# Projecting all queries, keys and gates ahead of the attention in a two-layer hybrid decoder trunk

## Chip, cores and metric

One NeuronCore of a Trainium2 chip runs the whole program. The metric is device time in microseconds (us), the median of several executions. PE is TensorE, PEld its weight load, DVE VectorE, ACT ScalarE, POOL GpSimd, SP SyncE. All tensors are float32; matmuls take their operands as fp32r pairs (below).

## Reference

Two layers (DEPTH 2) over x of 1024 tokens by 1024 channels. Each layer, cut to what matters:

```python
h = rmsnorm(x, pre_g)
fq, fk, fv, ff, fg, dq, dk, dv, dg, cb, cc, cx, cg, mg = split(h @ w_in)
# fox: 8 heads of 64, causal, with a running sum c of log_sigmoid(ff + b_f)
y_fox = softmax(fq fk^T / 8 + c_q - c_k) fv * silu(fg)
# diff: 4 heads, two maps of 64 each, the first 16 of 64 dims rotated by position
y_diff = rmsnorm((softmax_0 - lam * softmax_1) dv) * (1 - lam_init) * silu(dg)
# conv: 3 taps along the tokens
y_conv = cb * conv(cc * cx) * silu(cg)
g = sigmoid(mg + b_m)                      # three times 1024 channels
m = g0 * (y_fox @ w_fox) + g1 * (y_diff @ w_diff) + g2 * (y_conv @ w_conv)
x = x + rmsnorm(m @ w_o, post_g)
```

## The kernel before

A float32 operand is held as two fp32r tiles, hi and lo (ACT copies hi, POOL or DVE subtracts to get lo), and each product is three matmuls (mm3, L346). The columns of w_in come in chunks of 128. A plain chunk over all 1024 tokens takes two halves (h) of 8 steps in the depth, times three: 48 matmuls of 512 columns. A Strassen pair (strassen, L483) computes two chunks from seven products of 4 x 3 matmuls each, 84 in place of 96; build_s (L434) makes the sums s1 to s4 of the quarters of h that this needs, and emit_pair (L304) the sums of the weights. The order of products in strassen is a11, a12, s2, s3, s1, a22, s4; each product has its own PSUM bank, and a function use(j, h, x, ps, own) takes each of the four results.

Four groups of PSUM banks are S (3), T (2), O (1) and F (2); bank() cycles through all eight, pF through F alone. SBUF tiles of 4 KB a partition come from one pool of 41 blocks (blk), smaller ones from five tmps. SP issues nearly all loads, in the order in which the program has them; ACT's queue issues the stores and small copies. The framework orders the work of the other engines from the program order and its own estimates. A small clock (Clock, L62) delays steps by due times so that ACT and DVE steps come behind the matmuls they depend on.

A layer (L1145) runs so. conv_pair for the first two chunks of each conv tensor takes cc and cx plain and, while they run, build_s; all else of the conv is in pairs, and so are the merge gates mg and the gate fg. conv_merge (L579) makes the third branch's gate and multiplies it at once with y_conv @ w_conv into m0 in DRAM; gates_spilled (L604) writes the other gates to DRAM. One quarter of h (a21), overwritten by then, is reloaded. A first v_unit (L622, values for two pairs of heads, h stationary, 256 weight columns moving, 8 token blocks of 24 matmuls) and a first qk_unit (L702) follow, with forget (L657) for the sums c.

Then the attention (L1009): eight windows, one for each fox head pair (FOX_ORDER) and then for each diff head. A window's units go through the query groups g = 1, 2, 3, 0; stage1 (logits, softmax) of a unit alternates with stage2 (transposes, product with v) of the one before. Beside it, interleave (L122) spreads a filling over the window in proportion to its cost; PLAN (L39) lists it: the qk_unit and v_unit of later windows, plain; dg plain and unactivated (gate_raw); y_prep (L1041), which loads an attention output and its gate and multiplies and splits them; merge_br (L1069), which multiplies a branch with its weights and its gate. A qk_unit keeps its tiles in SBUF as stacks of hi over lo; swap (L761) copies the queries with halves exchanged for each unit by small DMAs on ACT's queue, and for diff the rotation exchanges rows by DMA and multiplies with tables on POOL and DVE.

Behind the attention come the merges left over (five of the first branch, eight of the second), then the output projection in two halves (out_half, out_rows), which also prepares the next layer's h.

## Time and profile before

| | |
|---|---|
| median of 3 runs | 2552.33 us (2551.42 to 2553.53) |
| the profiled execution's own time | 2547.05 us |
| its span, first to last instruction | 2545.2 us |
| mean granted TensorE clock | 0.986 |
| DRAM traffic | 264.61 MB, mean 104 GB/s |

The span starts at the first instruction. Layer 0 holds its attention from 583 to 1106 us, layer 1 from 1850 to 2372 us. Busy times are of the union of an engine's instructions; matmuls are pipelined, so that one of 512 columns has a duration of about 0.4 us while the next starts 0.23 us after it. Some matmul records can be missing.

### The profile page before, as it was taken

How to read it: one execution, taken by the hardware profiler on the slowest of the kernel's cores; microseconds unless marked ns; L12 is line 12 of the kernel's file. 1: busy time of each engine (PE TensorE's matmuls, PEld its weight loads, DVE VectorE, ACT ScalarE, POOL GpSimd, SP SyncE). 2: the span in 40 equal slices, each digit the busy share in tenths (PEclk: the TensorE clock that was granted, in tenths of full speed). 3: DMA queues.
4: the chain of work that ended last, by engine and by line, in shares of the span. 5: the costliest groups of instructions: out<-in, count | busy, mean ns of one | idle time of the engine just before them, and what ended most of it. 6: DMA issues, size and time to landing. Idle time of an engine off the chain costs nothing. (4 is left out here: it accounts for less than half of the span.)

```text
span 2545.2 us, 35790 instructions
## 1 busy us (share of the span) xinstructions
PE 2427.9 (95%) x13112; PEld 2043.0 (80%) x13112; DVE 1620.5 (64%) x2889; ACT 1109.7 (44%) x2290; POOL 859.8 (34%) x621
## 2 busy tenths in 40 slices
PE   7899999999999999899997999999999999999998
PEld 5677888888989787678976778888889887877798
DVE  6966464446566877677588664344465678777764
ACT  4224334336565555443432242233365655555333
POOL 1566324421122223361025662344211122234600
PEclk9899999999999999999998999999999999999999
DMA  4012223342222222654521122233322222226534
GB/s 168 33 50 95 92 95 116 104 138 70 62 75 73 73 84 74 192 203 138 194 95 42 50 91 96 75 106 118 121 72 62 77 70 81 75 83 207 206 117 182
DMA packets 113343, 264.61 MB, mean 104 GB/s; under 512 B 16128, under 2 KB 41088, under 8 KB 113168
## 3 DMA queue, kind: packets, MB, share of 16 engines
q1 hardware_dynamic: 57584, 187.52, 21.6%
q10 hardware_dynamic: 55584, 74.80, 9.5%
q8 instruction: 104, 1.70, 0.3%
q14 instruction: 71, 0.58, 0.1%
HBM read 187.68 MB, written 55.71 MB: 96 GB/s over the span
## 5 line engine op out<-in xcount | busy, mean ns | idle before, releaser
L279 POOL TENSOR_TENSOR wlo<-wraw,whi 128x1024 fp32r<-128x1024 f32 (+2 forms) x93 | 199.9, 2152 | 596.0 <-ACT whi L276 510.5
L351 PE MATMUL F<-ht,wlo 128*128 128x512 f32 x792 | 329.5, 416 | 0.0
L352 PE MATMUL F<-ht,whi 128*128 128x512 f32 x792 | 316.3, 399 | 0.0
L353 PE MATMUL F<-ht,whi 128*128 128x512 f32 x792 | 316.3, 399 | 0.0
L319 POOL TENSOR_TENSOR wlo<-sw,whi 128x512 fp32r<-128x512 f32 x160 | 225.3, 1419 | 225.8 <-ACT whi L318 200.2
L319 POOL TENSOR_TENSOR wlo<-wraw,whi 128x1024 fp32r<-128x1024 f32 x80 | 158.9, 1988 | 186.8 <-ACT whi L318 186.7
L318 ACT CAST whi<-sw 128x512 fp32r<-128x512 f32 x160 | 96.0, 620 | 248.3 <-DVE sw L321 107.2
L822 DVE TENSOR_TENSOR pt<-T,pt 128x512 fp32r<-128x512 f32 (+1 forms) x240 | 147.9, 633 | 47.1 <-ACT pt L821 45.5
L353 PEld LDWEIGHTS F<-ht,whi 128*128 128x128 f32 x792 | 150.0, 189 | 31.3
L352 PEld LDWEIGHTS F<-ht,whi 128*128 128x128 f32 x792 | 151.3, 191 | 25.1
L351 PEld LDWEIGHTS F<-ht,wlo 128*128 128x128 f32 x792 | 151.1, 191 | 24.7
L276 ACT CAST whi<-wraw 128x1024 fp32r<-128x1024 f32 (+2 forms) x126 | 117.9, 938 | 116.0 <-PE F L353 37.7
L783 PE MATMUL S<-qk,qk 128*128 128x512 f32 (+2 forms) x384 | 141.0, 367 | 20.6 <-ACT p L935 20.5
L821 ACT CAST pt<-T 128x512 fp32r<-128x512 f32 (+1 forms) x240 | 125.4, 544 | 75.1 <-PE T L174 55.3
L935 ACT ACTIVATE p<-S,sm 128x512 f32<-128x512 f32 (+2 forms) x192 | 110.6, 581 | 78.7 <-DVE sm L931 39.5
L929 DVE TENSOR_REDUCE sm<-S 128x1 f32<-128x512 f32 (+2 forms) x192 | 104.2, 550 | 45.7 <-PE S L787 23.1
L174 PE MATMUL T<-ident,p 128*128 128x128 f32 x864 | 129.5, 274 | 3.4 <-DVE p L946 3.2
L784 PE MATMUL S<-qk,sw 128*128 128x512 f32 (+2 forms) x384 | 130.7, 345 | 0.0
L318 ACT CAST whi<-wraw 128x1024 fp32r<-128x1024 f32 x80 | 66.8, 835 | 145.1 <-PE S L353 42.5
L351 PE MATMUL F<-whi,ht 128*128 128x256 f32 (+1 forms) x416 | 122.8, 295 | 3.9 <-DVE vd L373 3.9
L855 ACT ACTIVATE p<-p,sm 128x384 f32<-128x384 f32 (+7 forms) x128 | 99.5, 777 | 57.7 <-DVE sm L848 47.0
L321 DVE TENSOR_TENSOR sw<-wraw,sw 128x512 f32<-128x512 f32 x80 | 70.0, 875 | 82.4 <-POOL wlo L319 81.8
(393 smaller groups left out, 7168.5 us busy)
## 6 DMA issues: line engine op xcount, KB each, us to landing
wraw<-wt SPq DMA_DIRECT2D x128, 512.0 KB
mg<-tmp ACTq DMA_DIRECT2D x64, 256.0 KB
sw<-qk ACTq DMA_DIRECT2D x256, 64.0 KB
g<-mg SPq DMA_DIRECT2D x32, 512.0 KB
wraw<-wo SPq DMA_DIRECT2D x32, 512.0 KB
x<-x SPq DMA_DIRECT2D x24, 512.0 KB
wraw<-wbr SPq DMA_DIRECT2D x48, 256.0 KB
m<-tmp ACTq DMA_DIRECT2D x32, 256.0 KB
```

The lines of the kernel that those rows point to most:

```text
L174: self.nc.tensor.transpose(out, x, self.ident)
L276: nc.scalar.copy(hi, raw)
L279: getattr(nc, eng).tensor_tensor(out=lo, in0=raw, in1=hi.bitcast(F32), op=ALU.subtract)
L318: nc.scalar.copy(w[0][:, o], f)
L319: nc.gpsimd.tensor_tensor(out=w[1][:, o], in0=f, in1=w[0][:, o].bitcast(F32), op=ALU.subtract)
L351: nc.tensor.matmul(ps, wl, xh, start=start and i == 0, stop=False)
L352: nc.tensor.matmul(ps, wh, xl, start=False, stop=False)
L353: nc.tensor.matmul(ps, wh, xh, start=False, stop=stop and i == n - 1)
L783: nc.tensor.matmul(ps[:, :wp], q[:, i * P:(i + 1) * P], k[:, c0:c0 + wp], start=True, stop=False)
L784: nc.tensor.matmul(ps[:, :wp], qsw[:, (i % 2) * P:(i % 2) * P + P], k[:, c0:c0 + wp], start=False, stop=not last)
L821: self.clock.later(0.1, lambda: nc.scalar.copy(hi, T[:, n0:]))
L822: done = self.clock.later(0.6, lambda: nc.vector.tensor_tensor(out=lo, in0=T[:, n0:], in1=hi.bitcast(F32), op=ALU.subtract))
```

## The change

In a layer, the four v_units come first, plain, and go to DRAM (L.v); build_s is cut in two steps that stand between them, and forget and, in layer 0, setup_late (the rotation tables) between the last two. Then all queries, keys, gates and the conv are projected in Strassen pairs, 32 of them; conv pairs alternate with the others. qk_pair writes hi and lo of the scaled results to DRAM by head (L.qk), for diff with columns gathered so that the 16 rotated dims of all heads stand in chunk 0, the only one that is rotated; the rotation runs behind the next pair's start. The third merge gate and y_conv go to DRAM too. strassen adds two more products into banks already used: a12's into that of a11, a22's into that of s3, s4's into that of s1. conv_merge, qk_unit, stack_evac, gate_raw, swap and the reload of a21 are gone.

In the attention the windows' filling is now a load_pair for the next window (ten DMAs, 4.2 MB: queries, queries with halves exchanged, keys, values), merges of the conv branch (br 2, the result to DRAM), y_preps and merges of the fox branch (br 0, which load the partial sum and write it back). One merge of br 0 and eight of br 1 stand behind the attention. The diff, cut:

```diff
 PLAN = (
-    (("qk", "f", 3),),
-    (("qk", "f", 0), ("v", "f", 0)),
-    (("qk", "f", 1),),
-    (("qk", "d", 0), ("v", "d", 0)),
-    (("qk", "d", 1), ("dg", 0)),
-    (("qk", "d", 2), ("v", "d", 1)),
-    (("qk", "d", 3), ("y", "f", 0), ("dg", 2), ("y", "f", 1), ("dg", 1), ("y", "f", 2), ("y", "f", 3)),
-    (("dg", 3), ("br", 0), ("br", 1), ("br", 2)),
+    (("load", "f", 1), ("br", 2, 0), ("br", 2, 1)),
+    (("load", "f", 2), ("br", 2, 2), ("br", 2, 3), ("y", "f", 0)),
+    (("load", "f", 3), ("br", 2, 4), ("br", 2, 5), ("y", "f", 1)),
+    (("load", "d", 0), ("br", 2, 6), ("y", "f", 2)),
+    (("load", "d", 1), ("br", 2, 7), ("y", "f", 3), ("br", 0, 0)),
+    (("load", "d", 2), ("br", 0, 1), ("br", 0, 2)),
+    (("load", "d", 3), ("br", 0, 3), ("br", 0, 4), ("y", "d", 0)),
+    (("br", 0, 5), ("y", "d", 1), ("br", 0, 6)),
 )
-FILLS = {f for w in PLAN for f in w}
-COST = {"v": 20.8, "qk": 20.8, "dg": 10.4, "y": 1.0, "br": 5.2}
+COST = {"load": 0.0, "y": 1.0, "br": 5.2}
...
+            yield
...
-    def strassen(self, L, c0, c1, use, uv=None):
+    def strassen(self, L, c0, c1, use, scale=1.0):
...
+        def product(b, a, ps=None):
+            more = ps is not None
+            ps = ps or self.bank()
+            self.mm3(ps, [(w[b][0][:, k], w[b][1][:, k], *(t[:, k % 2] for t in L.a[a][k // 2])) for k in range(4)],
+                     not more, True, True)
             return ps
...
+        uv = self.blk([P, 2, 512], F32, "uv")
+        u, v = uv[:, 0], uv[:, 1]
+        p1 = product("b11", "a11")
+        nc.scalar.activation(u, p1, AF.Copy, scale=scale)
+        p6 = product("t2", "s2")
+        self.plus(u, u, p6, scale)
+        use(0, 0, None, product("b21", "a12", p1), False)
+        p7 = product("t3", "s3")
+        self.plus(v, u, p7, scale)
         p5 = product("t1", "s1")
-        nc.vector.tensor_tensor(out=u, in0=u, in1=p5, op=ALU.add)
-        use(1, 1, v, p5, False)
...
+        use(1, 1, v, p5, True)
+        use(0, 1, u, product("t4", "a22", p7), False)
+        use(1, 0, u, product("b22", "s4", p5), True)
+
+    def plus(self, o, x, ps, scale=1.0):
+
+        if scale == 1.0:
+            self.nc.vector.tensor_tensor(out=o, in0=x, in1=ps, op=ALU.add)
+        else:
+            self.nc.vector.scalar_tensor_tensor(out=o, in0=ps, scalar=scale, in1=x, op0=ALU.mult, op1=ALU.add)
...
+        pair = lambda name, use: self.strassen(L, (name, c), (name, c + 1), use)
+        pair("cc", use_cc)
+        yield
+        pair("cx", times(u))
...
+        yield
+        pair("cb", times(t))
+        yield
+        pair("cg", use_cg)
+        for j in range(2):
             hi, lo = self.blk([P, S], F32R, "ych"), self.blk([P, S], F32R, "ycl")
-            self.split(hi, lo, t, self.nc.gpsimd)
-            L.yc.append((hi, lo))
-
...
+            self.split(hi, lo, t[j], nc.gpsimd)
+            for x, o in enumerate((hi, lo)):
+                nc.scalar.dma_start(L.yc[c + j, x], o.bitcast(F32))
+        yield
...
+            if t % 4 == 3:
+                for j in range(2):
+                    self.clock.later(0.5, lambda j=j, h=h: nc.scalar.dma_start(
+                        L.v[kind][2 * u + j, h], vt[j][h].rearrange("p t a d -> p (t a d)").bitcast(F32)))
...
+    def qk_pair(self, L, kind, n, c):
+
+        nc = self.nc
+        scale = -0.125 if n == "q" else 1.0
+        dst = L.qk[kind, n]
+
+        def store(ch, h, t):
             sl = slice(h * 512, h * 512 + 512)
+            for x in range(2):
+                src, d = t[:, x].bitcast(F32), dst[x]
+                if kind == "f":
+                    nc.scalar.dma_start(d[2 * ch:2 * ch + 2, :, sl].rearrange("m d s -> (m d) s"), src)
+                elif ch:
+                    nc.scalar.dma_start(d[:, 16 * ch:16 * ch + 16, sl], src)
+                else:
+                    for r in range(2):
+                        nc.scalar.dma_start(d[:, 8 * r:8 * r + 8, sl],
+                                            src[64 * r:64 * r + 64])
+
+        def use(j, h, x, ps, own):
+            y = self.total(x, ps, own, scale)
+            t = self.blk([P, 2, 512], F32R, "hl")
+            if kind == "d" and c + j == 0:
+                if x is None:
+                    y = self.tmp()
+                    nc.scalar.activation(y, ps, AF.Copy, scale=scale)
+                xs = self.tmp()
+                for r in range(2):
+                    nc.scalar.dma_start(xs[64 * r:64 * r + 64], y[64 - 64 * r:128 - 64 * r])
                 rt = self.blk([P, 2, 512], F32, "rope")
+                sl = slice(h * 512, h * 512 + 512)
                 nc.sync.dma_start(rt[:, 0], self.rope_c[:, sl])
                 nc.sync.dma_start(rt[:, 1], self.rope_s[:, sl])
+
+                def rotate():
+                    nc.gpsimd.tensor_tensor(out=xs, in0=xs, in1=rt[:, 1], op=ALU.mult)
+                    nc.vector.tensor_tensor(out=y, in0=y, in1=rt[:, 0], op=ALU.mult)
+                    nc.vector.tensor_tensor(out=y, in0=y, in1=xs, op=ALU.add)
+                    self.split(t[:, 0], t[:, 1], y)
+                    store(c + j, h, t)
+
+                self.behind.append(rotate)
+                return
+            if x is None and scale != 1.0:
+                nc.scalar.activation(t[:, 0], ps, AF.Copy, scale=scale)
+                nc.vector.scalar_tensor_tensor(out=t[:, 1], in0=ps, scalar=scale, in1=t[:, 0].bitcast(F32),
+                                               op0=ALU.mult, op1=ALU.subtract)
+            else:
+                self.split(t[:, 0], t[:, 1], y)
+            store(c + j, h, t)
+
+        self.strassen(L, (kind + n, c), (kind + n, c + 1), use, scale)
...
+    def load_pair(self, L, kind, p):
+
+
+        nc = self.nc
+        L.q[kind, p], L.k[kind, p], L.vt[kind, p] = [], [], []
+        for e in range(2):
+            m = 2 * p + e
+            tiles = [self.blk([P, S], F32R, "qk") for _ in range(3)]
+            for t, n in zip(tiles, "qk"):
+                nc.sync.dma_start(t.bitcast(F32), L.qk[kind, n][:, m])
+            for x in range(2):
+                nc.sync.dma_start(tiles[2][64 - 64 * x:128 - 64 * x].bitcast(F32), L.qk[kind, "q"][x, m])
+            L.q[kind, p].append((tiles[0], tiles[2]))
+            L.k[kind, p].append(tiles[1])
         for h in range(2):
+            t = self.blk([P, 4, 4, 64], F32R, f"v{kind}")
+            nc.sync.dma_start(t.rearrange("p t a d -> p (t a d)").bitcast(F32), L.v[kind][p, h])
+            L.vt[kind, p].append(t)
+        L.done.add((kind, p))
...
-    def swap(self, qs, g):
-
-        nc = self.nc
-        s = self.sw(F32R)
-        gs = slice(g * 256, g * 256 + 256)
-        out = [s[:, i * 256:i * 256 + 256] for i in range(2)]
-        for t, q in zip(out, qs):
-            nc.scalar.dma_start(t[0:64].bitcast(F32), q[64:128, gs].bitcast(F32))
-            nc.scalar.dma_start(t[64:128].bitcast(F32), q[0:64, gs].bitcast(F32))
-        return out
...
-            nc.tensor.matmul(ps[:, :wp], qsw[:, (i % 2) * P:(i % 2) * P + P], k[:, c0:c0 + wp],
+            nc.tensor.matmul(ps[:, :wp], qsw[:, i * P:(i + 1) * P], k[:, c0:c0 + wp],
...
-            q, k, cb = L.qk["f", p][0][e], L.qk["f", p][1][e], L.cb[hd]
-            if e == 0:
-                L.fsw = self.swap(L.qk["f", p][0], g)
-            qsw = L.fsw[e]
+            (q, qsw), k, cb = L.q["f", p][e], L.k["f", p][e], L.cb[hd]
...
-            if raw:
-                later(0.0, lambda g1=g1: nc.scalar.activation(g1, g1, AF.Sigmoid))
-                later(0.6, mul)
-            later(1.0, lambda o1=o1, hi=hi: nc.scalar.copy(hi, o1))
-            y.append(later(1.6, lambda o1=o1, hi=hi, lo=lo: nc.gpsimd.tensor_tensor(
+            later(0.7, lambda o1=o1, hi=hi: nc.scalar.copy(hi, o1))
+            y.append(later(1.3, lambda o1=o1, hi=hi, lo=lo: nc.gpsimd.tensor_tensor(
                 out=lo, in0=o1, in1=hi.bitcast(F32), op=ALU.subtract)))
             yield 0.5
...
-        if br == 0:
+        if br != 2:
             mf = self.blk([P, S], F32, "mf")
-            nc.sync.dma_start(mf, L.m0[dc])
-            L.mf.append(mf)
+            nc.sync.dma_start(mf, L.m0[br][dc])
...
+        if br != 1:
+            self.clock.later(1.8, lambda: nc.scalar.dma_start(L.m0[0 if br == 2 else 1][dc], g))
...
+        self.behind = []
+        sums = self.build_s(L)
         run(self.v_unit(L, "f", 1, self.bank))
+        next(sums)
+        run(self.v_unit(L, "f", 0, self.bank))
+        run(sums)
         self.clock.flush()
-        decay = self.forget(L)
...
-        L.done = {("qk", "f", 2), ("v", "f", 1)}
+        run(self.v_unit(L, "d", 0, self.bank))
+        run(self.forget(L))
+        if l == 0:
+            self.setup_late()
+        run(self.v_unit(L, "d", 1, self.bank))
+        self.clock.flush()
+
+        def pairs(names, fn):
+            return [lambda n=n, c=c: fn(n, c) for n in names for c in (0, 2)]
+
+        qk = pairs(("fq", "fk", "dq", "dk"), lambda n, c: self.qk_pair(L, n[0], n[1], c))
+        silu = pairs(("fg", "dg"), lambda n, c: self.gates_spilled(L, (n, c), (n, c + 1)))
+        gates = [lambda c=c: self.gates_spilled(L, ("mg", c), ("mg", c + 1))
+                 for b in (16, 0, 8) for c in range(b, b + 8, 2)]
+        rest = qk + silu + gates
+        conv = chain([self.conv_pair(L, 0), self.conv_pair(L, 2)])
+        for n, job in enumerate(rest):
+            if n % 2 == 0:
+                next(conv, None)
+            self.run_behind()
+            if n == len(rest) - 2:
+                self.load_pair(L, "f", 0)
+            job()
+        run(conv)
+        self.load_yc(L)
...
-                p = FOX_ORDER[n]
-                units = [self.fox_unit(L, p, e, g) for g in G_ORDER for e in range(2)]
+                units = [self.fox_unit(L, n, e, g) for g in G_ORDER for e in range(2)]
...
+                if f[0] == "load":
+                    gens.append(self.loads(L, *f[1:]))
...
-                    gens.append(self.merge_br(L, 0, f[1], self.pF))
...
+                    gens.append(self.merge_br(L, f[1], f[2], self.pF))
...
+        for c in range(len(L.y["d"]), 4):
+            run(self.y_prep(L, "d", c))
+        done = {f for w in PLAN for f in w}
         for br in range(2):
...
+                if ("br", br, dc) not in done:
                     run(self.merge_br(L, br, dc, self.bank))
...
+    def chunk(n, c):
+        if n not in ("dq", "dk"):
+            return cols(OFF[n] + c * P, P)
+
+        m, d = np.arange(8), np.arange(16)
+        i = m[:, None] * 64 + c * 16 + d[None, :]
+        i = i.reshape(8, 2, 8).transpose(1, 0, 2) if c == 0 else i
+        return w[:, :, OFF[n] + i.reshape(-1)]
```

## Rows read from the trace of the kernel before

**Rows 1.** The page's part 1: busy us, share of the span, instructions.
```profile
PE 2427.9 (95%) x13112; PEld 2043.0 (80%) x13112; DVE 1620.5 (64%) x2889; ACT 1109.7 (44%) x2290; POOL 859.8 (34%) x621
```

**Rows 2.** Windows: stretch, length, each engine's busy us (instructions), granted clock, DMA share, GB/s.
```profile
250.00:500.00 250.00, 250.00 (x1083) 203.70 (x1082) 125.84 (x184) 94.96 (x137) 97.25 (x65) 1.00 0.30 103
...
75.00:250.00 175.00, 158.10 (x651) 126.02 (x651) 129.98 (x129) 54.36 (x80) 111.73 (x66) 0.96 0.16 57
1300.00:1500.00 200.00, 182.30 (x748) 145.84 (x747) 153.68 (x140) 58.23 (x84) 118.34 (x66) 0.94 0.16 55
```

**Rows 3.** Waits of PE, 75 to 250 us: who, for whom, us, times, longest.
```profile
PE F L351 <- POOL wlo L319: 5.4, 2, 3.4
PE S L351 <- ACT s L448: 5.1, 1, 5.1
```

**Rows 4.** Windows of the attention: single ones of layer 0, then the halves of both layers.
```profile
831.00:893.00 62.00, 59.24 (x319) 47.54 (x318) 51.27 (x118) 36.15 (x95) 15.65 (x16) 1.00 0.26 75
...
965.00:1046.00 81.00, 76.77 (x394) 62.48 (x393) 63.90 (x121) 40.93 (x103) 33.94 (x26) 0.98 0.40 117
1046.00:1106.00 60.00, 51.99 (x262) 40.22 (x261) 38.33 (x92) 28.04 (x78) 21.89 (x20) 0.94 0.55 181
...
583.00:831.00 248.00, 247.11 (x1636) 216.71 (x1635) 163.08 (x445) 146.56 (x326) 44.17 (x53) 1.00 0.25 72
831.00:1106.00 275.00, 255.87 (x1411) 208.88 (x1410) 207.17 (x451) 144.53 (x378) 88.13 (x77) 0.98 0.36 111
1850.00:2098.00 248.00, 246.65 (x1633) 216.32 (x1633) 162.95 (x445) 146.33 (x326) 43.65 (x51) 1.00 0.25 72
2098.00:2372.00 274.00, 256.12 (x1419) 210.26 (x1418) 207.94 (x452) 146.66 (x380) 88.21 (x77) 0.99 0.36 112
```

**Rows 5.** Timeline of PE in a v_unit: start, us, line, tile; eleven matmuls, first and last.
```profile
701.42 0.28 PE L352 MATMUL F<-wlo,ht 128*128 128x256 f32 x1
...
702.60 0.28 PE L353 MATMUL F<-whi,ht 128*128 128x256 f32 x1
```

**Rows 6.** DVE by line: the second window, the fifth, the last, then the run.
```profile
L699 DVE SCALAR_TENSOR_TENSOR qk<-F,qk 64x512 fp32r<-64x512 f32 x8 | 5.5, 689 | 0.9 <-ACT qk L698 0.7
...
L699 DVE SCALAR_TENSOR_TENSOR qk<-tmp,qk 64x512 fp32r<-64x512 f32 x8 | 5.5, 687 | 0.3
L732 DVE TENSOR_TENSOR tmp<-tmp,tmp 128x512 f32<-128x512 f32 x4 | 4.3, 1086 | 0.0
...
L728 DVE TENSOR_TENSOR tmp<-tmp,rope 128x512 f32<-128x512 f32 x4 | 2.7, 676 | 0.0
...
L1058 DVE TENSOR_TENSOR o<-o,g 128x512 f32<-128x512 f32 x5 | 3.3, 700 | 6.6 <-issue 6.6
...
L1058 DVE TENSOR_TENSOR o<-o,g 128x512 f32<-128x512 f32 x48 | 50.1, 1093 | 14.0 <-issue 6.6 <-DMA g<-fg 5.6 <-ACT g L1061 1.7
...
L1087 DVE TENSOR_TENSOR g<-g,F 128x512 f32<-128x512 f32 x26 | 17.6, 681 | 10.7 <-PE F L353 10.7
...
L373 DVE TENSOR_TENSOR vf<-F,vf 128x128 fp32r<-128x128 f32 x40 | 11.6, 289 | 17.3 <-ACT vf L372 17.0
```

**Rows 7.** Timeline of ACT in the fifth window: a DMA issue on its queue.
```profile
851.60 0.69 ACTq L723 DMA_DIRECT2D tmp<-tmp  x1
```

**Rows 8.** Windows: the merges behind the attention, layer 0 and layer 1.
```profile
1106.00:1186.00 80.00, 75.73 (x333) 61.40 (x332) 63.84 (x76) 29.71 (x47) 42.96 (x30) 0.98 0.58 205
2372.00:2449.00 77.00, 73.91 (x315) 59.68 (x314) 61.67 (x73) 26.75 (x45) 42.96 (x29) 0.96 0.56 203
```

**Rows 9.** Windows: two neighbouring stretches at the end of the attention of layer 0.
```profile
1040.00:1060.00 20.00, 18.00 (x87) 13.83 (x86) 9.34 (x21) 10.17 (x26) 11.15 (x11) 0.98 0.76 232
1060.00:1080.00 20.00, 15.09 (x73) 11.08 (x71) 14.87 (x39) 9.74 (x29) 3.27 (x4) 0.85 0.53 166
```

**Rows 10.** Waits of SP's queue over the run: who, for whom, us, times, longest.
```profile
SPq L878 <- DVE pt L822: 198.6, 4, 51.5
```

More of the change, by code (lines that the diff above doesn't have):

```diff
@@ L505, in plain @@
-    def plain(self, L, jobs):
-        for i in range(0, len(jobs), 3):
-            part = [(self.load_chunk(L.l, *c), use) for c, use in jobs[i:i + 3]]
-            for h in range(2):
-                for q, (w, use) in enumerate(part):
-                    if (i, h, q) == (3, 0, 0):
-                        self.build_s(L)
-                    use(h, self.proj(w, h))
-    def total(self, x, ps, own):
+        def product(b, a, ps=None):
[3 more added lines that the diff above has]
+                     not more, True, True)
+            return ps
@@ L1001, in stage2 @@
             later(2.0, out)
[L1003 to L1007 removed]
+        return stage1, stage2, 2 * W1D * (4 * g + 3) + W2D * (g + 1), {("d", hd)}
     def attention(self, L, windows):
@@ L1024, in attention @@
         fill = windows[0][1]
-        for _ in range(3):
-            next(fill, None)
         run(stage1(0))
@@ L1142, in out_rows, with run_behind, loads @@
                 nc.scalar.dma_start(self.x1[(h * 4 + tb) * P:(h * 4 + tb + 1) * P, :], xt)
+    def run_behind(self):
+        jobs, self.behind = self.behind, []
+        for fn in jobs:
+            fn()
+    def loads(self, L, kind, p):
+        self.load_pair(L, kind, p)
+        yield 0.0
     def layer(self, l):
@@ L1164, in layer @@
-        gates = [(n, c) for n in ("mg", "fg", "dg") for c in range(16 if n == "mg" else 4) if (n, c) not in FILLS]
-        gates = list(zip(gates[::2], gates[1::2]))
-        for pair in gates[:2]:
-            self.gates_spilled(L, *pair)
-        late = self.setup_late() if l == 0 else iter(())
-        for dc in range(0, 8, 2):
-            if dc >= 4:
-                next(late, None)
-            self.conv_merge(L, dc)
-        run(late)
-        for pair in gates[2:]:
-            self.gates_spilled(L, *pair)
```

196 lines of the change are left out of this document (37 added, 159 removed).

## Prediction

> **What bounds the kernel now.** I read the page's first line first: TensorE (PE) is busy 2427.9 of 2545.2 us, VectorE (DVE) 1620.5, ScalarE (ACT) 1109.7 [rows 1]. So PE's work decides, but a share over the whole run hides the stages; the stretches come next. In the steady part of the projections PE issues 1083 matmuls in 250 us, 0.23 us each, with DVE at half load [rows 2]: a matmul saved there is worth 0.23 us. Early in each layer PE falls short: 651 instructions in 175 us and 748 in 200 us, where 0.23 us each would need 150 and 172 us [rows 2]; it waits there for the splits of weights and of the Strassen sums [rows 3]. Then the attention, 248 + 275 = 523 us in layer 0 and 248 + 274 = 522 us in layer 1. Its eight windows show two regimes: in the four fox windows PE is busy 247 of 248 us with DVE at 66%; in the fifth and the seventh DVE is at 83 and 79% and PE falls 3 to 4 us short [rows 4]. That is the row to remember: projections inside the attention give PE something to do while the softmax chain is under way.
>
> **Part 1: matmuls removed.** Per layer 24 chunks are plain (4 in the first conv_pair, 16 queries and keys, 4 dg), 48 matmuls each. As 12 Strassen pairs of 84 they lose 12 x 12 = 144 matmuls, 288 in all: 66 us at 0.23 us. Nothing else on PE changes in count. The 66 us are the whole prize; the rest is a question of where work lies.
>
> **Part 2: the attention gets shorter, and poorer in filling.** What leaves it in a layer: seven qk units of 96 matmuls less the 18 already issued ahead of it (654), four dg chunks (192), three merges (72), so 918 x 0.23 = 211 us; and three v units of 192 matmuls of 256 columns at (702.60 - 701.42)/10 = 0.118 us [rows 5], 68 us. What comes in: 15 merges of 24 matmuls, 360 x 0.23 = 83 us. By PE alone 523 - 196 = 327 us. Now the same for DVE. It is busy 163 + 207 = 370 us there [rows 4]. Leaving: three f units of 8 x 0.689 = 5.5 us; four d units of 5.5 + 4.3 + 2.7 = 12.5 us; three v units of 16 x 0.29 = 4.6 us, together 80 us [rows 6]. Coming: 12 more merges of 2 x 0.68 us and two more y_prep of 2 x 0.70 us, 19 us [rows 6]. Left: 309 us. DVE would have to be busy 95% of 327 us, which no stretch of the attention shows. The fifth window has 51.27 of 62 us, 83%, at full speed of the rest; the seventh 63.90 of 81, 79%, also with transfers in its way [rows 4]. Against these stands what goes: the swaps (16 small DMA issues a window) and the rope exchange, each holding ACT's queue up to 0.7 us [rows 7], and GpSimd's large weight splits, beside which DVE's SBUF operations stretch (the multiply at L1058: 1.09 us over the run, 0.70 us in the last window, where POOL does less [rows 6]). I take 88%, near the good end because that traffic goes: 309/0.88 = 351 us. Ends: 327 us (PE alone) and 309/0.79 = 391 us. Gain: 172 + 171 = 343 us, between 391 and 263.
>
> **Part 3: the stage before the attention gets longer.** Per layer it loses the plain conv (192 matmuls), conv_merge's own matmuls (192), one plain qk unit and the 18 matmuls ahead (114), and its pairs go from 20 to 32: 2688 against 2178, +510 x 0.23 = 117 us. Three v units come in, 68 us. +185 us a layer, +371 us in all, if PE runs at its steady pace. Does cover hold? A pair takes PE 84 x 0.23 = 19.3 us; in the steady row DVE, ACT and POOL are busy 126, 95 and 97 of 250 us [rows 2], so splits, the new scaled copies and stores (each 0.3 to 0.7 us of ACT's queue) fit. The banks p1, p7 and p5 are now written again; each reader has one product between, 12 x 0.23 = 2.8 us, against a read of 0.7 us. If DVE came later than that, 64 pairs would each pay; at 0.7 us apiece 45 us. The stalls early in the layer (25 + 28 us, from rows 2) should shrink: build_s now has three v units (68 us of PE) beside it rather than a stage that already used DVE for 130 of 175 us. I take two thirds of them, -35 us; ends 0 and -53. Against that: v_unit on the first half of the rows offers PE 96 x 0.118 = 11 us before the second half must be there, where three plain chunks offered 72 x 0.23 = 17 us, so up to 5 us a layer, I take 5 in all; and setup_late comes as one block, 3 us (ends 0 and 10). forget keeps its place in the chain and its cost.
>
> **Part 4: behind the attention.** Nine merges instead of thirteen: 4 x 24 x 0.23 = 22 us less per layer of the 80 and 77 us [rows 8]. But only one merge of the first branch (5.5 us) is left to cover the way of the last head's output through DRAM, where five covered it; y_prep has one multiply fewer. +3 us a layer (ends 0 and 8). Together -38 us.
>
> **Traffic.** Everything now goes through DRAM. In the attention an estimate from the diff: seven pair loads of 4.2 MB, rows of c 4.2, gates, weights and partial sums of the merges 23, y_prep 8, outputs 4: 70 MB in 351 us, 200 GB/s. The stretch behind the attention already runs at 205 GB/s and 58% [rows 8], so it fits, without much room.
>
> **The sum.** -343 + 371 - 35 + 5 + 3 - 38 = -37 us. The profiled execution took 2547.05 us with its span of 2545.2; the median of the three runs is 2552.33. From the median: 2515 us.
>
> **Rivals.**
> *PE alone sets the attention.* With DVE rid of stretched operations 327 us a layer holds: 2 x 24 us better, 2466 us. For it: in the fox windows PE is hardly ever idle [rows 4]. Against: they had 22 to 45 us of filling each for 25 to 30 us of attention; now it is 5 to 11 us.
> *The softmax chain sets the attention, and the kernel gets slower.* If the windows run at the seventh's 79% of DVE, the attention takes 391 us a layer, 2 x 40 us more than I said: 2595 us. It decides from 351 + 37/2 = 370 us, DVE at 83.5%, which is just above what the fifth window reached with more filling. For it: one S bank in three is held until ACT's exponential is done, and the remaining filling comes in two pieces a window.
> *The gate queues behind the pair.* SP issues load_pair first, then the gate of the window's first merge. 4.2 MB at the 232 GB/s of [rows 9] are 18 us; the first merge's half is done some 3 us into the window, so DVE, which takes its instructions in order, could stand 15 us at the multiply and the banks would fill behind it. In all 14 windows 210 us, 2725 us; it decides from three of them (37/15). Against: that multiply never waited for its gate, its idle time is all PE's; only y_prep's waited for one, 5.6 us over the run [rows 6]. SP's queue does stand: 198.6 us at the cB load, for a block to come free [rows 10]. The Trainium skill, DMA: Bandwidth & Descriptors, section "Queues, rings and completion order", says that SP has one ring on each DMA engine and that descriptors are taken in ring order, which speaks for this rival; no row here shows a gate late because of it.
> *The clock falls.* In the window stretch 1060 to 1080, after PE had been busy 18 of 20 us, it was busy 15 of 20 and the granted clock was 0.85, a mix of 2.4 and 1.2 GHz; over the last window it was 0.94 [rows 9, 4]. If all of the attention ran at 0.94, 6% of 351 us twice would be lost, 42 us: 2557 us, no change. The Trainium skill, TensorE: Matmul & The Clock Gate, section "Why this matters for your kernels", warns of idle stretches between bursts of matmuls, since the engine then drops to half its clock; by that the thinner filling costs as this rival says, and by the row of the fifth window (clock 1.00 at 95% busy) nothing. I sum with nothing.
> *The change does not do what it says*: the saved matmuls come back as waits for re-used banks, the 45 us above. It would lie between no change and the slower case, and is counted there.
>
> **How the numbers follow.** My forecast, 2480 to 2547 us: 0.50. PE alone, below 2480: 0.17. No change, the clock or the banks: 0.09. The softmax chain: 0.17. The gate: 0.07. About 0.2% (5 us) is what a measurement of this kernel can tell, so faster is 0.67, same 0.09, slower 0.24. The range 2450 to 2590 leaves out the lower end of the PE case (0.05), the upper end of the chain case (0.08) and the gate (0.07).
>
> **What would show it.** Right: 288 fewer matmuls of 512 columns; a stage before the attention of some 750 us in layer 0, PE full after the first 120; attention windows of about 40 us (fox) and 47 us (diff), DVE between 85 and 90% in them; DRAM traffic near 200 GB/s there. Wrong: windows over 46 us on average with DVE under 83% (chain); DVE or PE waiting for a DMA at the merges (gate); granted clock under 0.95 through the attention; PE waiting for DVE or ACT inside strassen. My weakest number is the 88%: two points of it are 16 us.

## The result, and the profile after

The changed kernel takes 3298.61 us (median of four, 3291.04 to 3302.33) against 2552.93 us in the same session: 1.292 times as long (95% interval 1.289 to 1.294). I had forecast 2515 us, within 2450 to 2590. Sign and size are both wrong.

The page of the changed kernel: busy time by engine, the bytes moved, and the group with the longest idle time on DVE.

```profile
PE 2478.9 (75%) x12824; PEld 2048.8 (62%) x12824; DVE 1590.5 (48%) x2897; ACT 1085.9 (33%) x2292; POOL 920.5 (28%) x677
...
HBM read 271.56 MB, written 127.01 MB: 121 GB/s over the span
...
L1045 DVE TENSOR_TENSOR g<-g,F 128x512 f32<-128x512 f32 x69 | 46.1, 678 | 452.5 <-DMA g<-mg 444.8
```

The 288 matmuls are gone, as counted (13112 to 12824, [rows 1]). PE is idle a quarter of the time, and one multiply, a merge's product by its gate, stands 445 us for the gate's load.

To see where, I cut both kernels at the first and the last score matmul (S) of each attention. Windows: stretch, length, busy us of each engine (instructions), granted clock, DMA share, GB/s. The last stretch, behind the attention of layer 1, stands in the table alone. First after:

```profile
0.00:832.40 832.40, 750.12 (x3528) 618.52 (x3529) 435.71 (x570) 274.01 (x468) 367.48 (x232) 0.97 0.37 125
832.40:1492.80 660.40, 340.15 (x1854) 269.65 (x1853) 284.14 (x766) 216.07 (x551) 77.53 (x94) 0.74 0.34 105
1492.80:2463.20 970.40, 897.55 (x4562) 752.21 (x4562) 496.41 (x652) 323.70 (x589) 381.38 (x244) 0.97 0.39 133
2463.20:3124.90 661.70, 339.33 (x1856) 269.66 (x1855) 284.52 (x767) 215.96 (x551) 77.77 (x95) 0.75 0.35 105
```

The same stretches of the kernel before:

```profile
0.00:583.00 583.00, 547.49 (x2442) 446.27 (x2443) 346.15 (x439) 209.93 (x321) 252.87 (x156) 0.99 0.28 98
583.00:1090.20 507.20, 488.29 (x2961) 413.68 (x2960) 359.63 (x873) 283.94 (x683) 126.78 (x124) 0.99 0.31 91
1090.20:1849.60 759.40, 726.28 (x3598) 608.03 (x3597) 439.98 (x542) 263.56 (x454) 304.93 (x187) 0.98 0.31 109
1849.60:2354.40 504.80, 486.67 (x2960) 413.46 (x2959) 359.21 (x873) 284.04 (x683) 126.65 (x124) 0.99 0.30 92
```

My sum, put on these borders (in the attentions 507.2 - 172 and 504.8 - 171; each stage ahead +185.5 - 17.5 + 2.5, the first +3 more; -19 behind each attention), beside what was measured. The columns e3, e6 and e5 are experiments below.

| stretch | before | forecast | after | e3 | e6 | e5 |
|---|---|---|---|---|---|---|
| ahead, layer 0 | 583.0 | 756.5 | 832.4 | 787.4 | 784.0 | 786.7 |
| attention, layer 0 | 507.2 | 335.2 | 660.4 | 460.6 | 396.7 | 366.6 |
| between | 759.4 | 910.9 | 970.4 | 922.2 | 921.6 | 924.0 |
| attention, layer 1 | 504.8 | 333.8 | 661.7 | 462.6 | 403.4 | 368.4 |
| behind | 190.8 | 171.8 | 171.4 | 170.9 | 171.4 | 171.0 |
| span | 2545.2 | 2508.2 | 3296.3 | 2803.7 | 2677.1 | 2616.7 |

Of the 788 us between forecast and result 653 lie in the two attentions and 135 ahead of them. PE and DVE together are far from full there: PE 340 and DVE 284 of 660 us, at 105 GB/s. Something that is neither work nor volume sets the time. The waits name it: who waits for whom, us, times, longest; PE, then DVE, then ACT.

```profile
PE F L349 <- DVE g L1045: 439.6, 13, 49.0
PE S L747 <- ACT p L896: 130.2, 12, 33.8
...
DVE g L1045 <- DMA g<-mg: 445.6, 12, 49.5
...
DVE sm L901 <- ACT p L896: 132.6, 16, 33.3
...
DVE sw L318 <- DMA wraw<-wt: 63.2, 7, 28.5
...
ACT whi L273 <- DMA wraw<-wbr: 580.8, 18, 49.3
```

It is one chain: the gate and the weights of a merge come late; DVE and ACT stand at them in their own order, and the exponentials and bank reads behind them stand too. And why late? SP's queue in the first window of layer 0: start, us, instruction (L721, L723 and L728 are load_pair; L268 a merge's weights; L1033 its gate).

```profile
829.08 0.55 SPq L721 DMA_DIRECT2D qk<-qf  x1
...
830.57 11.95 SPq L723 DMA_DIRECT2D qk<-qf  x2
...
843.24 10.92 SPq L721 DMA_DIRECT2D qk<-kf  x1
854.25 11.78 SPq L723 DMA_DIRECT2D qk<-qf  x2
866.12 3.24 SPq L728 DMA_DIRECT2D vf<-vf  x2
869.46 1.71 SPq L268 DMA_DIRECT2D wraw<-wbr  x1
871.26 1.59 SPq L1033 DMA_DIRECT2D g<-mg  x1
```

The gate is issued 42 us after the pair's first load, because three of these rows hold SP 11 to 12 us each. That is not so elsewhere: 53 of SP's 591 DMA issues take more than 4 us in this run, 48 of them for queries and keys, and none of 407 does in the kernel before. And in the middle of that, with every compute engine at rest:

```profile
850.00:860.00 10.00, 0.00 (x0) 0.00 (x0) 0.00 (x0) 0.00 (x0) 0.00 (x0) 0.50 0.18 57
```

57 GB/s with nothing but loads from SP's queue under way, where the merges of the kernel before ran at 205 [rows 8]. The DMA share of 0.18 is 2.9 of 16 engines. So these loads are slow by themselves, not for want of bandwidth; why, the experiments must show.

Two theories go from here. *Narrow*: load_pair reads both halves of a head's queries in one DMA, from a source of shape 2 x 64 x 1024 into 128 partitions, and that shape uses few engines. *Order*: the loads are as fast as others, but too much stands in SP's queue ahead of the merges (my rival "the gate queues behind the pair").

The Trainium skill, DMA: Bandwidth & Descriptors, section "Why a DMA increments its semaphore by 16 and not by 1", says that a transfer is spread over the largest number of engines, up to 16, that divides the slowest dimension other than 1 of both its sides; for a slowest dimension of 2 that is two engines. By it the narrow theory holds, and the 2.9 engines of the row lie near it (two for the narrow loads; the pair's loads of 64 partitions, which are not of that shape, stand between them). No row here counts the engines of one load.

### The profile page after: what moved, and what is told of

Its sections match the earlier page's. It is cut to its first block, busy times and chain, and to the rows that moved or that the text cites. A ratio compares the mean times of both kernels' runs of the same rounds, so it can differ in the third digit from the quotient of the medians.

```text
span 3296.3 us, 35531 instructions
## 1 busy us (share of the span) xinstructions
PE 2478.9 (75%) x12824; PEld 2048.8 (62%) x12824; DVE 1590.5 (48%) x2897; ACT 1085.9 (33%) x2292; POOL 920.5 (28%) x677
## 5 line engine op out<-in xcount | busy, mean ns | idle before, releaser
L316 POOL TENSOR_TENSOR wlo<-sw,whi 128x512 fp32r<-128x512 f32 x256 | 351.1, 1382 | 399.4 <-ACT whi L315 399.1
L276 POOL TENSOR_TENSOR wlo<-wraw,whi 128x512 fp32r<-128x512 f32 (+2 forms) x61 | 100.9, 1656 | 1052.1 <-ACT whi L273 1021.4
L316 POOL TENSOR_TENSOR wlo<-wraw,whi 128x1024 fp32r<-128x1024 f32 (+1 forms) x128 | 239.0, 1867 | 340.3 <-ACT whi L315 338.2
L315 ACT CAST whi<-wraw 128x1024 fp32r<-128x1024 f32 (+1 forms) x128 | 107.0, 836 | 316.9 <-issue 107.9
L349 PE MATMUL S<-s,wlo 128*128 128x512 f32 x448 | 179.1, 400 | 10.0 <-POOL wlo L316 8.8
L747 PEld LDWEIGHTS S<-qk,qk 128*128 128x128 f32 x384 | 80.4, 209 | 164.1 <-ACT p L896 140.9
L351 PE MATMUL S<-s,whi 128*128 128x512 f32 x448 | 178.6, 399 | 0.0
L350 PE MATMUL S<-s,whi 128*128 128x512 f32 x448 | 177.9, 397 | 0.0
L349 PE MATMUL T<-ht,wlo 128*128 128x512 f32 x384 | 154.3, 402 | 30.5 <-ACT uv L491 30.2
L351 PE MATMUL T<-ht,whi 128*128 128x512 f32 x384 | 152.3, 396 | 0.0
L350 PE MATMUL T<-ht,whi 128*128 128x512 f32 x384 | 151.4, 394 | 0.0
L172 PEld LDWEIGHTS T<-ident,p 128*128 128x128 f32 x864 | 104.0, 145 | 63.2 <-DVE p L907 53.8
```

The source lines that it names most:

```text
L172: self.nc.tensor.transpose(out, x, self.ident)
L276: getattr(nc, eng).tensor_tensor(out=lo, in0=raw, in1=hi.bitcast(F32), op=ALU.subtract)
L315: nc.scalar.copy(w[0][:, o], f)
L316: nc.gpsimd.tensor_tensor(out=w[1][:, o], in0=f, in1=w[0][:, o].bitcast(F32), op=ALU.subtract)
L349: nc.tensor.matmul(ps, wl, xh, start=start and i == 0, stop=False, skip_group_check=more)
L350: nc.tensor.matmul(ps, wh, xl, start=False, stop=False, skip_group_check=more)
```

## The experiments

**e1: the same loads, each cut in two.** Each q or k load becomes two of 64 x 1024; order, bytes and tiles are kept.

```
-                nc.sync.dma_start(t.bitcast(F32), L.qk[kind, n][:, m])
+                for x in range(2):
+                    nc.sync.dma_start(t[64 * x:64 * x + 64].bitcast(F32), L.qk[kind, n][x, m])
```

> The changed kernel, but load_pair's four loads of queries and keys (512 KB each, of shape 2 x 64 x 1024 in DRAM) are issued as two loads of 64 x 1024 each; same bytes, same order, same queue. Theory N (a load whose outermost dimension is 2 runs on two of the sixteen DMA engines; the changed kernel moved 57 GB/s at 850 to 860 us with all compute engines idle): a load_pair falls from some 45 us to under 20 us, the waits of DVE for g<-mg fall from 446 us to under 60 us, the attention to 350 to 400 us a layer, the run to 2520 to 2640 us. Theory O (4.2 MB ahead of the gate in one queue is what costs, however wide): 18 us a load stay, 15 us in each of 14 windows, 2725 us or more.

Measured: 2836.46 us, 1.111 times before (1.110 to 1.113): 462 of the 747 us of loss go. SP's queue around the same load, its wait, and the stretch that had moved 57 GB/s:

```profile
849.27 1.09 SPq L722 DMA_DIRECT2D qk<-qf  x2
850.72 10.69 SPq L722 DMA_DIRECT2D qk<-kf  x2
861.50 1.19 SPq L724 DMA_DIRECT2D qk<-qf  x2
...
871.80 0.43 SPq L1034 DMA_DIRECT2D g<-mg  x1
```

The row of 10.69 us is two issues and a wait between them; SP's waits from 826 to 880 us have it:

```profile
SPq L722 <- DMA of<-tmp: 13.1, 2, 9.3
```

```profile
850.00:860.00 10.00, 9.84 (x69) 8.40 (x68) 6.08 (x20) 5.89 (x19) 0.57 (x2) 1.00 0.64 189
```

From the pair's first load to the gate it is now 22.5 us instead of 42, and of these SP only waits for 13.1; no issue of this run takes more than 4 us. The stretch has a DMA share of 0.64, with other transfers beside the pair's. But the time lands between the two theories' ranges, and the waits show what is left:

```profile
PE F L349 <- DVE g L1046: 122.3, 13, 15.0
...
DVE g L1046 <- DMA g<-mg: 130.2, 12, 15.5
```

As many waits as before, 15 us at the longest where it was 49. That is the size that my rival had priced, but the price came from bytes (4.2 MB at 232 GB/s), and here 13.1 of 22.5 us are SP's waits between its loads: the order is the rival's, the number is in part luck. The narrow loads made the wait three times as long.

**e2: the narrow loads, but last in each window.** The changed kernel with load_pair moved behind the merges of its window, unsplit. It asks whether the narrow loads cost anything where no merge stands behind them.

```
-    (("load", "f", 1), ("br", 2, 0), ("br", 2, 1)),
+    (("br", 2, 0), ("br", 2, 1), ("load", "f", 1)),
```

> The changed kernel with its loads as they are, but in each window of PLAN the load of the next pair stands behind the merges instead of ahead of them. Theory N: DVE no longer waits for the gates of the same window, but a load still takes 45 us and now begins late, so the next window's first logits wait for it; 3000 to 3400 us, with PE waiting for the transfers at the logits. Theory O: the gates are ahead in the queue, the waits are gone, 2515 to 2640 us.

Measured: 3172.35 us (a single execution). The gate's waits are gone and the score matmuls wait for the queries and keys themselves:

```profile
PE S L747 <- DMA qk<-kf: 203.9, 12, 23.5
PE S L747 <- DMA qk<-kd: 144.3, 9, 23.7
```

So order alone is not the cause: the narrow loads cost wherever they stand. From e1 and e2 together, narrowness is the largest part.

**e3: e1, and a bank for each product.** Splits the loads and gives strassen back a bank for each of its seven products, with the sums on DVE that this needs, as in the kernel before but with the scale. Three of the products of the changed kernel add into a bank already used (not two, as the change's description says). It prices this re-use that I had summed with nothing and bounded at 45 us.

```
-        use(0, 0, None, product("b21", "a12", p1), False)
+        use(0, 0, u, product("b21", "a12"), False)
...
-        use(1, 1, v, p5, True)
-        use(0, 1, u, product("t4", "a22", p7), False)
-        use(1, 0, u, product("b22", "s4", p5), True)
+        self.plus(u, u, p5, scale)
+        use(1, 1, v, p5, False)
+        use(0, 1, v, product("t4", "a22"), True)
+        use(1, 0, u, product("b22", "s4"), True)
```

> As e1_split_loads, and strassen with a bank for each of its seven products, as in the kernel before (seven additions on DVE a pair in place of five). If the re-used banks cost what the trace of the changed kernel shows at 150 to 740 us (PE waits of 9.8 us for ACT's copy of p1 and some 2 us for DVE in a layer), 20 to 25 us less than e1_split_loads; if these waits only stand where PE would wait anyhow, within 8 us of it; if DVE's two more additions a pair (88 us over the run) come on the path, slower than it.

Measured: 2806.01 us, 1.100 (1.098 to 1.102), 30.5 us less than e1. DVE works 103 us more over the run (1699.2 against 1596.4) and the run is still shorter. Re-use cost 30 us over 64 pairs, 0.48 us a pair. The runs e4 to e6 start from e3.

**e4: e3 with the first merge of each window ahead of the load.**

```
-    (("load", "f", 1), ("br", 2, 0), ("br", 2, 1)),
+    (("br", 2, 0), ("load", "f", 1), ("br", 2, 1)),
```

> The kernel of e3 (split loads, a bank for each product) with one change: in each window the first merge, with its weights and its gate, is issued ahead of the load of the next pair, not behind it. E3's time is 2806. If the order in SP's queue is what is left of the loss, the waits of the multiply for its gate (128 us of DVE, 119 of PE) and half of the waits of ACT for the merge's weights go, and the second merge's gate, now the one behind the load, has some 20 us until it is needed: 2630 to 2700. If it is the volume of the loads, the wait only moves on to the second merge or to the logits that need the pair: 2770 to 2820. If it is the softmax chain that sets the windows, within 30 us of 2806 as well, but with PE waiting for the exponential and not for a load.

Measured: 2786.27 us, 1.091 (1.089 to 1.093): 20 us, not the 100 to 180 of the order theory.

```profile
POOL o L1008 <- DMA rb<-rs: 176.7, 6, 41.0
...
PE S L746 <- DVE sm L811: 41.3, 7, 22.3
...
DVE g L1044 <- DMA g<-mg: 94.8, 12, 10.9
...
ACT whi L273 <- DMA wraw<-wbr: 133.5, 16, 13.2
```

The gate's wait fell from 128 to 95 us and the weights' from 180 to 134; it moved on to the second merge, which now stands behind the load. And the edit brought a wait of its own: in the fourth and fifth window the y_prep now follows right behind the load, with no merge between (the first row is GpSimd at y_prep's multiply; four of its six waits are 37 to 41 us). The fifth window grows from 71.3 to 86.7 us in layer 0 and from 72.6 to 86.1 in layer 1, while the other seven of a layer lose 23 and 22 us together. So the 20 us understate what the order costs, and this left open whether queue order or the bytes of the loads were at work; e5 and e6 part them.

**e5: e3 with one pair loaded a layer.** All windows use the first pair's tiles, so the seven later loads of a layer are left out; the arithmetic stays. This is the attention without the traffic of the pairs.

```
+        if (kind, p) != ("f", 0):
+            for d in (L.q, L.k, L.vt):
+                d[kind, p] = d["f", 0]
+            L.done.add((kind, p))
+            return
```

> The kernel of e3 with the load of a pair made only once in a layer: all eight windows take the queries, keys and values of the first fox pair, and the seven later loads (29 MB a layer) are left out, with the waits of the queue that they bring. All arithmetic stays. The attention of layer 0 takes 510 us in e3. If the loads, by volume or by order, are what is left of the loss, it falls to 350 to 390 us a layer, the length that the prediction gave it, and the run to some 2500 to 2580. If the softmax chain or the clock sets the windows, it stays at 450 to 500 us and the run at 2700 to 2790.

Measured: 2618.18 us, 1.026 (1.024 to 1.028). Loads in any form account for 188 us of e3, and without them the changed kernel is still slower than before. The windows of layer 0: the four fox windows, then the four diff windows one by one.

```profile
786.70:948.00 161.30, 155.77 (x1008) 131.53 (x1006) 122.05 (x367) 106.45 (x237) 29.79 (x47) 1.00 0.38 122
948.00:1010.90 62.90, 46.07 (x222) 34.12 (x221) 44.12 (x110) 30.41 (x87) 16.16 (x16) 0.84 0.31 105
1010.90:1052.70 41.80, 37.74 (x211) 28.22 (x210) 36.79 (x96) 25.97 (x76) 9.78 (x9) 1.00 0.26 89
1052.70:1098.10 45.40, 40.30 (x226) 30.43 (x224) 38.74 (x98) 25.51 (x75) 7.87 (x11) 1.00 0.35 122
1098.10:1153.30 55.20, 41.63 (x194) 32.67 (x194) 43.50 (x98) 27.56 (x78) 14.19 (x12) 0.81 0.23 82
```

Here is my forecast's attention at last: fox windows of 40 us (PE busy 97% of them and DVE 76%, so that PE sets them and not DVE, as I had it), and a sixth and seventh of 42 and 45 us with DVE busy 88 and 85%. But the fifth and the eighth take 63 and 55 us, DVE at 70 and 79%, at a clock of 0.84 and 0.81.

**e6: e3 with the loads issued by GpSimd.** Same bytes, same place in the program, another queue.

```
-                    nc.sync.dma_start(t[64 * x:64 * x + 64].bitcast(F32), L.qk[kind, n][x, m])
+                    nc.gpsimd.dma_start(t[64 * x:64 * x + 64].bitcast(F32), L.qk[kind, n][x, m])
```

(and likewise the swapped queries and the values)

> The kernel of e3 with one change: the 14 loads of a pair are issued by GpSimd, in its own DMA queue, and not by SP; order in the program, tiles and bytes are the same. E3 took 2806 us, and with seven of the eight loads of a layer left out it took 2618. If the 188 us between them are the order in SP's queue (the merges' weights and gates stand behind 14 loads that wait for a block each), the waits for gate and weights (119 of PE, 128 of DVE, 180 of ACT in e3) go and the time comes to 2620 to 2700. If they are the bytes themselves (the 16 DMA engines shared by 4.2 MB a window and all the rest), gates and weights come as late as before, from another queue: 2770 to 2830. Against both: GpSimd has its own work in the attention, some 8 of 50 us, and each wait for a block now stands in front of that; it would show as PE or DVE waiting for a GpSimd instruction.

Measured: 2682.86 us, 1.053 (1.050 to 1.055), 123 us less than e3, with 175 GB/s in the attention of layer 0 where e3 had 151. Waits for gates and merge weights are nearly gone (DVE 8.5 us where it was 128, ACT 26.5 where it was 180); in their place PE waits for a small GpSimd instruction (a memset) that stands behind the loads in GpSimd's order:

```profile
PE O L855 <- POOL pt L778: 32.9, 6, 8.7
```

So of the 188 us at least 123 are the order in SP's queue, its waits ahead of loads included, not bytes. The 65 us up to e5 lie in the fox windows (190 us against 161 in layer 0). GpSimd's standing is part of them; how much is the bytes stays open.

**e7: one part alone, in the kernel before: dg in pairs.** The four dg chunks leave the attention and go through Strassen pairs ahead of it.

```
-    (("qk", "d", 1), ("dg", 0)),
+    (("qk", "d", 1),),
-    (("qk", "d", 3), ("y", "f", 0), ("dg", 2), ("y", "f", 1), ("dg", 1), ("y", "f", 2), ("y", "f", 3)),
-    (("dg", 3), ("br", 0), ("br", 1), ("br", 2)),
+    (("qk", "d", 3), ("y", "f", 0), ("y", "f", 1), ("y", "f", 2), ("y", "f", 3)),
+    (("br", 0), ("br", 1), ("br", 2)),
```

> One part of the change alone, in the kernel before: the four dg chunks of a layer leave the attention and are projected in two Strassen pairs ahead of it, their gates spilled; queries, keys, values and merges stay where they were. It takes 24 matmuls a layer away, 48 in all (11 us at 0.23), and 192 matmuls a layer out of the filling of the fifth, seventh and eighth window. If thin filling as such is cheap (as it is in the kernel of e3 without the loads, where the fox windows ran at 48 to 50 of 50 us of PE), 2540 to 2552. If the diff windows need their filling (they reached 83 and 79% of DVE with it, and are the windows where PE still idles in e3 without the loads), the saved matmuls come back as waits for the softmax chain: 2555 to 2590.

Measured: 2622.10 us, 1.028 (1.026 to 1.030): 70 us slower with 48 matmuls fewer, beyond both ranges. The first score matmul comes 41.5 us later (624.5 against 583.0), the price of two pairs; the attention takes 504.9 us from first to last score matmul where it took 507.2. The diff windows (a window's border is its first of 48 score matmuls), e7:

```profile
865.80:915.00 49.20, 46.68 (x252) 37.78 (x252) 38.54 (x94) 28.39 (x76) 11.94 (x10) 0.97 0.21 58
915.00:1003.50 88.50, 75.40 (x442) 64.76 (x441) 65.83 (x144) 43.36 (x113) 22.12 (x21) 0.90 0.24 66
1003.50:1059.30 55.80, 51.10 (x284) 40.94 (x282) 43.79 (x100) 32.23 (x87) 12.32 (x12) 0.97 0.16 45
1059.30:1129.40 70.10, 51.03 (x224) 36.72 (x225) 51.94 (x106) 31.59 (x83) 33.90 (x29) 0.78 0.59 190
```

and the kernel before:

```profile
824.20:881.30 57.10, 54.51 (x305) 44.20 (x304) 47.22 (x110) 34.86 (x89) 18.17 (x16) 1.00 0.22 63
881.30:956.00 74.70, 70.40 (x438) 59.78 (x437) 56.45 (x129) 39.26 (x104) 16.75 (x16) 1.00 0.30 89
956.00:1032.00 76.00, 71.77 (x386) 59.63 (x385) 57.60 (x112) 38.89 (x98) 25.90 (x18) 0.98 0.29 85
1032.00:1090.00 58.00, 51.09 (x251) 39.04 (x251) 39.87 (x94) 29.40 (x80) 24.64 (x24) 0.94 0.65 207
```

192 matmuls left these windows, 44 us at 0.23, and only 2 us came back: 8 and 20 us less in the fifth and seventh, 14 and 12 more in the sixth and eighth (15 and 15 in layer 1). The sixth had lost no matmul; why it grew is not shown beyond its clock. Work beside the diff windows had cost next to nothing where it stood, and costs its full time where it went. The granted clock fell in each (1.00, 1.00, 0.98, 0.94 to 0.97, 0.90, 0.97, 0.78), so that part of the time came back as slower matmuls: PE is busy 75.4 us for 442 instructions in the sixth where it was 70.4 for 438.

**e8: the reverse, in the kernel before.** Two merge gate chunks a layer move from a pair ahead into the fifth and the eighth window.

```
-    (("qk", "d", 1), ("dg", 0)),
+    (("qk", "d", 1), ("dg", 0), ("mg", 14)),
-    (("dg", 3), ("br", 0), ("br", 1), ("br", 2)),
+    (("dg", 3), ("br", 0), ("br", 1), ("br", 2), ("mg", 15)),
```

(merge_br applies the sigmoid to the two)

> The reverse of the change, in the kernel before: two merge gate chunks a layer leave their Strassen pair ahead of the attention and are projected plainly beside the diff windows (one in the fifth, one in the eighth), spilled raw; the merge behind the attention applies their sigmoid. It adds 12 matmuls a layer (96 plain for 84 of a pair), 24 in all, and takes 84 x 0.23 = 19 us a layer from the stage ahead. Theory: the diff windows are set by the softmax chain, and matmuls beside them cost less than their time (the run with the dg chunks taken out of them showed no shorter attention). PE is busy 262.7 of 281.8 us there in the kernel before, so 19 of the 22 us that come in could hide: 2515 to 2548. Rival: PE's idle time there cannot be filled (it lies at the end of windows, behind transfers and the last exponential), the attention grows by the whole 22 us a layer, and the run takes 2551 to 2565.

Measured: 2567.01 us, 1.006 (1.004 to 1.008), just above the rival's range. The first score matmul comes 14.4 us earlier, and the attention takes more than that back, 24 us in layer 0 and 27 in layer 1, half of it in the fifth window:

```profile
810.30:879.80 69.50, 65.68 (x358) 53.17 (x357) 52.09 (x116) 37.61 (x93) 22.13 (x18) 1.00 0.29 82
```

69.5 us for 57.1, with 48 matmuls (11 us) more. Of the filling of these windows, then, what was taken out (e7) saved next to nothing, and what was added (96 matmuls a layer, 22 us) cost its full time.

**e9: e6 with the four merges of the fifth and eighth windows multiplied twice.** The second product is written over the first.

```
+            if (br, dc) in TWICE:
+                self.mm3(z, prods)
+                self.clock.tick(2.6)
+                yield 2.6
             self.mm3(z, prods)
```

> The kernel of e6 (split loads on GpSimd's queue, 2683 us) with the product of four merges a layer made twice, the second over the first: the two merges beside the fifth window and the two beside the eighth. It adds 96 matmuls a layer (22 us at 0.23) where the matmuls that the change took away had stood, and nothing else; the output is the same. These two windows take 63.3 and 55.1 us in layer 0 of e6, with PE busy 45 of 63 in the fifth at a granted clock of 0.86. If matmuls there lie in time that the softmax chain leaves, and keep the clock up besides, the run stays within 10 us of 2683 and the clock of the fifth window rises over 0.90. If PE is the bound there after all, the two windows grow by 22 us a layer and the run takes 2715 to 2735.

Measured: 2696.58 us, 1.058 (1.056 to 1.060): 14 us more for 192 matmuls (44 us), so two thirds hid; neither range holds it. The fifth, sixth and eighth window of layer 0:

```profile
979.90:1042.90 63.00, 51.40 (x243) 39.04 (x242) 44.29 (x108) 29.71 (x86) 23.24 (x31) 0.81 0.59 172
1042.90:1094.20 51.30, 44.09 (x234) 34.46 (x234) 36.70 (x99) 26.34 (x77) 18.89 (x25) 0.93 0.57 155
1140.50:1191.80 51.30, 46.04 (x241) 36.04 (x240) 41.81 (x95) 27.65 (x78) 13.66 (x14) 0.93 0.31 107
```

The eighth as it was in e6:

```profile
1125.60:1180.70 55.10, 41.69 (x195) 32.63 (x196) 43.45 (x98) 27.65 (x78) 14.38 (x13) 0.80 0.28 100
```

The fifth keeps its length (63.3 us in e6) and its clock does not rise (0.87 in e6); by the counts about half of its extra matmuls ran in the sixth, which grows from 42.0 to 51.3 us. The eighth is the other way: with 46 more matmuls its clock rises from 0.80 to 0.93 and it gets 4 us shorter (55.7 to 52.2 us, 0.79 to 0.93, in layer 1). So most of these matmuls lie in time that something other than PE sets, and there a thin window can get shorter by more work. Why the fifth is longer than the sixth and seventh stays open.

## Why the prediction was wrong

The way from result to forecast, in medians: 3299 after; 462 for narrow loads (2836, e1); 30 for the re-used banks (2806, e3); 123 for the order in SP's queue (2683, e6); 65 for the rest of the loads (2618, e5); 103 that are no matter of the later pairs' loads (2515, forecast). Each share holds for this order of edits; in another they would come out otherwise.

*Traffic: the failing step.* I set 70 MB against 205 GB/s and found that it fits. That compares volumes, and takes for granted that a new load runs as the old ones do. None of the old loads had the shape of these: the diff shows a source of 2 x 64 x 1024, and I read it as 512 KB. The volume was near enough (105 GB/s in 660 us is 69 MB), and the attention of e6 moved 175 GB/s. The rate of one load in its own shape was what I never asked for; e1, which changes only that, puts its cost at 462 us, some 397 of them in the two attentions.

*The rival "the gate queues behind the pair".* The right mechanism, with its place: the multiply at the gate, DVE in order, banks filling behind it. Its price was 15 us a window at 232 GB/s; e1 shows 15.0 and 15.5 us at the longest, and 130 us in all where I had 210, with more than half of the way to the gate, in the window shown, spent in SP's waits; e6 takes 123 us out by moving the loads. As run, the load was narrow and the wait 49 us. My argument against it, that this multiply had never waited for its gate, could not count: in the kernel before nothing of 4.2 MB stood ahead of that gate. With a chance of 0.07 it was dismissed on a row that could not speak of it.

*Part 2: 88% of DVE.* DVE's work was near: 284 us between first and last score matmul, where my 309, less the 10 that lie outside these borders (370 - 359.6), gives 299. The share was wrong. Without the pairs' loads (e5) DVE is busy 285.2 of 366.6 us, 78%, the share of the rival "the softmax chain" (79% of [rows 4]). The sixth and seventh window reach 88 and 85%, the fifth and eighth do not, and the fox windows are at 76% because PE sets them; I carried one share through all of them. These are 31 and 35 of the 108 us of span between forecast and e5.

*Part 3: the stage ahead.* In layer 0 it takes 786.7 us in e5 against my 756.5, in layer 1 13 us too much. PE's idle time was to shrink by 35 us over both; from the windows of before it is 35.5 and 33.1 us, in e5 46 (786.7 - 740.77) and 36. It grew: "build_s beside v" is the term that failed. From 50 to 150 us PE is busy 85.4 of 100 us in e5 (84.5 in the kernel as changed) and 87.7 before, so none of PE's idle time there went, where I had counted on two thirds; and from 150 us on another 14.5 us are idle in e5, where it was 7.5 before. The kernel as changed takes another 46 us in each of the two stretches. Re-used banks (taken at nothing, bound 45, measured 30 over both) are some 15 of each. The other 31 are the first pair's narrow loads, which SP issues ahead of the last pairs' weights (DVE waits for such weights up to 28.5 us in the rows above): in e1 the first score matmul comes at 801.7 us where it came at 832.4, and the stretch between the attentions takes 938.5 us where it took 970.

*Part 1: a prize that was not there.* I took 0.23 us for each matmul saved wherever it stood. That holds ahead of the attention, where PE is full. The chunks in the diff windows gave next to nothing back when they left: e7 saves 48 matmuls and loses 70 us. Whether they had been hidden beside the softmax chain, or the lower clock took back what they freed, no run parts. With all 288 gone, PE is busy 2425.8 us in e5 against 2427.9 before, not 66 less.

*The clock.* The rival named 0.94 for the attention; e5 has 0.94 in both, after 0.74 and 0.75. It goes with PE's idle time in most windows here: 1.00 in e5's fox windows (97% busy), 0.84 in its fifth (73%), 0.80 in e6's eighth (76%) and 0.93 in e9's (90%). The busy share alone does not tell it: e9's fifth has 0.81 at 82%. I had summed with nothing. Its own price cannot be parted from the waits that bring it. The Trainium skill, TensorE: Matmul & The Clock Gate, section "Why this matters for your kernels", warns of such idle stretches between matmuls; e5's and e9's eighth windows (0.81 at 75% busy, 0.93 at 90%) agree.

*What held.* The count of matmuls; DVE's work in the attention (5% under); the stretch behind (171.4 us, forecast 171.8); and fox windows of 40 us once the loads are away, though not for the reason that I gave.

No run beats the kernel before. The plan without its later loads (e5, which leaves out what a right answer needs) is 2.6% above it, one part alone (e7) 2.8%, and its reverse (e8) 0.6%.

## What to carry to other kernels

Price a new transfer by its own shape, from a row with that shape, and look at what stands behind it in its queue; bytes over bandwidth say only what can't be beaten. Before work is moved out from beside a latency chain, ask what it costs where it stands: work that hides there (two thirds of what e9 added) has little price, and its full price elsewhere; and filling put back can lift a clock that was low without it (e9's eighth window). And an argument "this never waited" counts only if the thing it would now wait for was there.

## What the runs showed of the hardware

A 512 KB load with a leading dimension of two moved 57 GB/s alone at a DMA share of 0.18; cut into two of 64 partitions, with other transfers beside them, the same stretch ran at 189 GB/s and 0.64, and the cut alone was worth 462 us here. The cost was also on SP: 53 of its 591 DMA issues took 4 to 12 us, most of them of the pairs' queries and keys, those of 64 partitions that stand behind a narrow load too; after the cut none of 655 did. The granted clock lay at 0.50 in a stretch without matmuls (of the two levels the lower, 1.2 GHz), and at 0.74 to 0.85 over attentions whose PE was busy 51 to 74% of the time (the kernel as changed, e3).
